# Where the column-half sums of the second chunk's attention outputs are formed, in a four-stage decoder step

## The chip, the cores and the metric

The kernel runs on one core of one Trainium2 chip. The metric is device time in microseconds (us) of one execution. A core has a matrix engine (TensorE, PE in the profile, with PEld for its weight loads), a vector engine (VectorE, DVE), a scalar engine (ScalarE, ACT), GpSimd (POOL), which here mainly issues stores, and SyncE (SP), which here issues loads. The engines run side by side and wait for each other through semaphores.

## The reference, cut to what matters

One inference step for 1024 prompt positions and 8 decode positions, model width 2048, all in fp32:

```
layer A:  u, gate = x @ w_in_a;  d = pool(u) per group @ w_grp
          y = (d * scale * silu(gate)) @ w_out_a;   x = LayerNorm(ALPHA*x + y)
k, v = x @ w_kv
layer B:  q, gate = x @ w_in_b;  o = windowed attention with sinks(q, k, v)
          y = (o * silu(gate)) @ w_out_b;           x = LayerNorm(ALPHA*x + y)
```

The change concerns the gated attention output `o * silu(gate)` of layer B, on its way into the product with `w_out_b`.

## The kernel before

**Tiles and stages.** Activations lie transposed: 128 channels on the partitions, 16 channel tiles side by side, positions along the free dimension. There are two chunks of positions: chunk 0 has 512, chunk 1 has 520, of which the last 8 are the decode positions. The stages run in the order ai (input product of layer A), ao (output product), bi (K, V, query and gate products and attention) and bo (output product of layer B), each for chunk 0 and then chunk 1. `bi` of chunk 1 is followed by `bo` of chunk 0 and that by `bo` of chunk 1, the last stage.

**Products.** Nearly all large products are made in Strassen's way (Winograd's form) with seven products of half size in place of eight: `seven` (L565), its `run` (L619) and the three matmuls of L641 to L643. Each operand is split into a rounded high part (a cast on ACT: L474 for weights, L752 for activations) and a low part (a subtraction on DVE: L489 for weights, L761 for activations); the three matmuls are high times high, high times low and low times high. One product is 24 matmuls, and PE needs its low weights at its third matmul. A stage is 56 products (seven for each of eight pairs of output tiles), and the first two pairs of `bo` share their activations product by product (`both`).

**The activations' sums.** Of the seven activation operands, three are halves of the columns as they are (numbers 0, 4 and 5), and four (1, 2, 3 and 6) are sums and differences of an even channel tile E and an odd one O, each cut into a first column half a and a second column half b:

```python
nc.vector.tensor_sub(t[:, 1, :], E[:, a], E[:, b])
nc.vector.tensor_sub(t[:, 2, :], E[:, b], O[:, b])
nc.vector.tensor_add(t[:, 0, :], O[:, b], t[:, 1, :])
nc.vector.tensor_sub(t[:, 3, :], O[:, a], t[:, 0, :])
```

This is `t_ops` (L803; the four operations are L809 to L812), which also issues the store of the result to a buffer in device memory, `Td`, from POOL (L813; `to` in the profile for these outputs). At the start of the next stage `x_load` (L726, issue L742) loads operands from `act` (`o`) and `Td` (`to`), `x_cast` (L745) makes the high part and `x_make` (L755) the low one. For chunk 0, whose columns are all prompt positions, the gate of an odd tile calls `t_ops` on the two tiles still held in memory. For chunk 1 it can't at once: the half of 260 columns ends with decode columns 512 to 519, which come from another path. So `gate` (L1825) only stores the tile (L1831) and gives its buffer back, and when `bo` of chunk 0 has run 18 products a generator, `t_gen` (L816), starts: it loads the 16 stored tiles again, two at a time (L822), and calls `t_ops` eight times, once a product or less. Its loads, sums and stores thus lie in `bo` of chunk 0. When `bo` of chunk 1 is prepared (`x_begin`, L683, called when the seventh of the eight pairs starts), `ready` runs what is left of the generator to its end.

**Decode columns.** `decode` (L1882) makes the attention of the 8 decode positions for eight tiles at a time; its last step `s9` (L1960, issue L1966) multiplies with the gate values `sgd` and stores 8 columns for 8 tiles.

**Order.** The whole instruction order is written out when the program is made. `begin` (L501) loads, casts and prepares weights some products ahead, as set by `ahead`; `end` (L513) runs the events due after a product (`at` and `product` put them there), the steps of the activations (`x_tick`, L768) and one step of a side generator. PE, DVE and ACT run their instructions in this order, and so do the queues of SP and POOL. There are 53 full buffers (`Mem`, L135), each of which can serve as two halves; `full` hands out the one that was given back longest ago, so the first write to a buffer can wait for a store that still reads it. A second generator, `sum_gen` (L400), makes the sums of `w_out_b` in `bi` of chunk 1 (adds L422, L426 and L427, store L428 of `swob`); it takes a new piece only with more than five free buffers. In `bi` of chunk 1 the prefetch shrinks while fewer than four buffers are free (L504). For two of the eight weight pairs of `bo` chunk 0 the sums are made on the spot (`first_pair`, adds L332).

**The end.** `phase_end` (L1291) uses a small tile `four` for the last four columns of a half.

## Time and profile before

| | |
|---|---|
| median of 3 runs | 2367.28 us (2366.43 to 2371.67) |
| the profiled execution | 2367.62 us, of which the profile's span is 2365.9 us |
| PE busy in the span | 2326.4 us (98%) |
| DVE / ACT / POOL busy | 1923.5 / 1342.2 / 201.5 us |
| granted TensorE clock, mean | 0.996 |
| `t_gen`'s loads of `o` (L822, SP) | x8, first issued at 2063.8, last at 2119.8 |
| stores of `to` (L813, POOL) for both chunks | x16, first issued at 1238.0, last at 2132.8 |

Times on the engines count from the span's start. A row of a group has busy time and the mean of one instruction; a row of waits has the engine and line that waited, the line it waited for, the sum in us, how often, and the longest. A row of a timeline has start, duration, engine, line and operation, and in brackets the idle time ahead of it and what ended that. "PE busy" is modelled from matmul starts, so idle PE is what can be told apart from it.

### The profile page before, as it was taken

To read this page: it belongs to the slowest core of one execution; us is meant where nothing else is said; L and a number is where in the kernel's file an instruction comes from. 1 tells how busy PE (TensorE), PEld (TensorE's weight loads), DVE (VectorE), ACT (ScalarE), POOL (GpSimd) and SP (SyncE) were. 2 spreads that over 40 slices of the span, in tenths; PEclk is the share of its full clock that TensorE was granted. 3 is DMA by queue.
4 is the path that set the end of the run, shared out by engine and by line. 5 is a ranking of instruction groups with operands and counts; after the bars stand their busy time and mean duration, and the time that the engine had idled before them with its cause. 6 is when DMAs were issued, how large, how long until landed. Compare 5 with 4: busy or idle time off the path is not lost. (4 is left out here: it accounts for less than half of the span.)

```text
span 2365.9 us, 46542 instructions
## 1 busy us (share of the span) xinstructions
PE 2326.4 (98%) x18424; PEld 2219.4 (94%) x18424; DVE 1923.5 (81%) x2385; ACT 1342.2 (57%) x2429; POOL 201.5 (9%) x379
## 2 busy tenths in 40 slices
PE   8999999999999999999999999999999999999997
PEld 6899999999999999998778899999999999999997
DVE  8787998776878878868888888887777768888887
ACT  4444446544536547554554656685666667546556
POOL 0111110001000000000111111100000000000000
PEclk9999999999999999999999999999999999999999
DMA  8678789889889989989888766788787768699785
GB/s 294 215 244 303 274 291 349 308 308 315 286 278 365 331 270 324 334 314 330 282 324 322 258 230 224 238 297 275 232 259 221 222 193 298 227 353 371 259 302 194
DMA packets 252059, 669.18 MB, mean 283 GB/s; under 512 B 25760, under 2 KB 106560, under 8 KB 251840
## 3 DMA queue, kind: packets, MB, share of 16 engines
q1 hardware_dynamic: 206368, 501.14, 64.0%
q0 software_dynamic: 45472, 165.07, 17.9%
q8 instruction: 144, 2.36, 0.4%
q14 instruction: 75, 0.61, 0.1%
HBM read 471.01 MB, written 185.59 MB: 278 GB/s over the span
## 5 line engine op out<-in xcount | busy, mean ns | idle before, releaser
L641 PE MATMUL pD<-m,m 128*128 128x260 f32 (+1 forms) x4752 | 1346.9, 283 | 9.9 <-DVE m L602 3.7
L643 PE MATMUL pD<-m,m 128*128 128x260 f32 (+1 forms) x4752 | 1340.5, 282 | 4.5 <-DVE m L489 4.5
L642 PE MATMUL pD<-m,m 128*128 128x260 f32 (+1 forms) x4752 | 1340.3, 282 | 0.0
L641 PEld LDWEIGHTS pD<-m,m 128*128 128x128 f32 x4752 | 896.0, 189 | 21.0 <-issue 10.2
L643 PEld LDWEIGHTS pD<-m,m 128*128 128x128 f32 x4752 | 896.7, 189 | 6.0 <-DVE m L489 6.0
L642 PEld LDWEIGHTS pD<-m,m 128*128 128x128 f32 x4752 | 896.3, 189 | 0.5
L489 DVE TENSOR_TENSOR m<-m,m 128x1024 fp32r<-128x1024 f32 x674 | 814.1, 1219 | 96.1 <-ACT m L474 58.3
L474 ACT CAST m<-m 128x1024 fp32r<-128x1024 f32 x674 | 701.6, 1048 | 305.2 <-DVE m L332 71.3
L669 PE MATMUL pD<-m,m 128*128 128x512 f32 x448 | 179.7, 401 | 8.0 <-ACT m L752 8.0
L670 PE MATMUL pD<-m,m 128*128 128x512 f32 x448 | 177.2, 396 | 0.5 <-DVE m L761 0.5
L671 PE MATMUL pD<-m,m 128*128 128x512 f32 x448 | 177.2, 396 | 0.0
L761 DVE TENSOR_TENSOR m<-m,m 128x1024 fp32r<-128x1024 f32 (+1 forms) x120 | 146.9, 1225 | 7.2 <-ACT m L752 5.7
L614 ACT COPY m<-pD 128x260 f32<-128x260 f32 (+1 forms) x83 | 31.0, 373 | 188.2 <-PE pD L643 188.1
L752 ACT CAST m<-m 128x1024 fp32r<-128x1024 f32 (+1 forms) x120 | 125.7, 1052 | 14.2 <-PE pD L670 5.2
L669 PEld LDWEIGHTS pD<-m,m 128*128 128x128 f32 x448 | 84.7, 189 | 29.9 <-ACT m L752 8.0
L332 DVE TENSOR_TENSOR m<-m,m 128x1024 f32<-128x1024 f32 x88 | 107.6, 1222 | 5.9 <-DMA m<-in_wia 4.2
L670 PEld LDWEIGHTS pD<-m,m 128*128 128x128 f32 x448 | 84.8, 189 | 20.4 <-DVE m L761 1.6
L671 PEld LDWEIGHTS pD<-m,m 128*128 128x128 f32 x448 | 84.6, 189 | 19.8
L602 DVE TENSOR_TENSOR m<-pD,m 128x260 f32<-128x260 f32 (+1 forms) x86 | 36.4, 424 | 81.9 <-PE pD L643 78.6
L1778 ACT ACTIVATE m<-m,sm 128x128 f32<-128x128 f32 x256 | 99.2, 390 | 0.0
L1071 PE MATMUL pD<-m,m 128*128 128x260 f32 (+1 forms) x528 | 91.5, 323 | 0.0
L607 DVE TENSOR_TENSOR m<-pD,m 128x260 f32<-128x260 f32 (+1 forms) x84 | 35.6, 424 | 64.2 <-PE pD L643 64.0
(243 smaller groups left out, 2167.3 us busy)
## 6 DMA issues: line engine op xcount, KB each, us to landing
m<-in_wia SPq DMA_DIRECT2D x124, 512.0 KB
m<-in_wib SPq DMA_DIRECT2D x120, 512.0 KB
swia<-m POOLq DMA_DIRECT2D x64, 512.0 KB, 4.9
m<-swia SPq DMA_DIRECT2D x64, 512.0 KB
m<-swoa SPq DMA_DIRECT2D x64, 512.0 KB
swib<-m POOLq DMA_DIRECT2D x64, 512.0 KB, 5.3
m<-swib SPq DMA_DIRECT2D x64, 512.0 KB
m<-swob SPq DMA_DIRECT2D x56, 512.0 KB
```

Source lines behind the costliest of these rows:

```text
L332: self.nc.vector.tensor_add(s[out].a[:, :1024], s[x].a[:, :1024], s[y].a[:, :1024])
L474: self.nc.scalar.copy(hi.r[:, :1024], self.stream[self.cast].src().a[:, :1024])
L489: self.nc.vector.tensor_sub(lo.r[:, :1024], s.src().a[:, :1024], hi.a[:, :1024])
L641: nc.tensor.matmul(ps[:, :TH], wh[:, s], h, start=new and k == 0, stop=False, skip_group_check=on)
L642: nc.tensor.matmul(ps[:, :TH], wh[:, s], l, start=False, stop=False, skip_group_check=on)
L643: nc.tensor.matmul(ps[:, :TH], wl[:, s], h, start=False, stop=k == 7, skip_group_check=on)
L669: nc.tensor.matmul(ps[:], wh[:, s], h, start=par == 0 and k == 0, stop=False)
L670: nc.tensor.matmul(ps[:], wh[:, s], l, start=False, stop=False)
L671: nc.tensor.matmul(ps[:], wl[:, s], h, start=False, stop=par == 1 and k == 7)
L752: self.nc.scalar.copy(h.r[:, :n], s.a[:, :n])
L761: self.nc.vector.tensor_sub(l.r[:, :n], s.a[:, :n], h.a[:, :n])
L1778: nc.scalar.activation(x["s3"][:, i, :], x["s3"][:, i, :], AF.Exp, bias=nm[:, i : i + 1], scale=0.125, accum_out=rs[:, i : i + 1],)
```

## The change

The generator for chunk 1's attention outputs is no longer added. In its place:

- `gate` of chunk 1 keeps the even tile's half buffer until the odd tile is done, and one product after the odd tile's gate it calls `t_ops` on both, over all 520 columns. Columns 512 to 519 of each tile are set to zero first (a memset on POOL), so the last 8 of the 260 columns of each sum are not the wanted ones.
- `gate` also copies columns 252 to 259 of each tile (the last 8 of the first half) into a new tile `oa` (an ACT copy).
- `o_dec`: when all eight gates of a group of tiles and its `decode` are done, four small DVE operations form the sums of those 8 columns alone, from `oa` and `sgd`, into a new tile `otd`, one product later.
- `x_cast`, for the operands 1, 2, 3 and 6 of this input, copies `otd` over the last 8 columns of the loaded tile (an ACT copy) before the cast.
- `four` in `phase_end` becomes a part of `oa`.

```diff
+TROW = {1: 0, 2: 1, 3: 2, 6: 3}
...
+        self.oa = one.tile([P, NH // 2, NDEC], F32, name="oa")
+        self.otd = one.tile([P, NK // 2, 4, NDEC], F32, name="otd")
+        self.odn = {}
...
         h = self.mem.full()
+        if self.xkey == ("o", 1) and k[0] in TROW:
+            t = s.v(4, THM)[:, :, THM - NDEC : THM]
+            self.nc.scalar.copy(t, self.otd[:, 4 * k[1] : 4 * k[1] + 4, TROW[k[0]], :])
         self.nc.scalar.copy(h.r[:, :n], s.a[:, :n])
...
-        four = self.small(NK * 4, 1)
-        f3 = four[:].rearrange("p (k t) -> p k t", k=NK)
+        four = self.oa[:].rearrange("p k t -> p (k t)")[:, : NK * 4]
+        f3 = four.rearrange("p (k t) -> p k t", k=NK)
...
             nc.gpsimd.dma_start(self.act["o", c][:, t, :TP], a.a[:, :TP])
             if c == 1:
-                self.ao.pop((c, t)).free(True)
-            elif t % 2:
+                nc.gpsimd.memset(a.a[:, TP:T], 0.0)
+                nc.scalar.copy(self.oa[:, t, :], a.a[:, THM - NDEC : THM])
+                self.o_dec(t // 8)
+            if t % 2:
                 e = self.ao.pop((c, t - 1))
-                self.t_ops(e.a[:, :TP], a.a[:, :TP], self.Td["o", c], t // 2, T // 2)
-                e.free(True)
-                self.ao.pop((c, t)).free(True)
+
+                def sums():
+                    self.t_ops(e.a[:, :T], a.a[:, :T], self.Td["o", c], t // 2, T // 2)
+                    e.free(True)
+                    self.ao.pop((c, t)).free(True)
+
+                if c == 1:
+                    self.at(1, sums)
+                else:
+                    sums()
...
+    def o_dec(self, pr):
+
+        self.odn[pr] = self.odn.get(pr, 0) + 1
+        if self.odn[pr] < 9:
+            return
+
+        def go():
+            nc = self.nc
+            d, o = self.sgd[pr][:], self.oa[:, 8 * pr : 8 * pr + 8, :]
+            Ea, Oa, Eb, Ob = o[:, 0:8:2, :], o[:, 1:8:2, :], d[:, 0:8:2, :], d[:, 1:8:2, :]
+            t = self.otd[:, 4 * pr : 4 * pr + 4]
+            nc.vector.tensor_sub(t[:, :, 1, :], Ea, Eb)
+            nc.vector.tensor_sub(t[:, :, 2, :], Eb, Ob)
+            nc.vector.tensor_add(t[:, :, 0, :], Ob, t[:, :, 1, :])
+            nc.vector.tensor_sub(t[:, :, 3, :], Oa, t[:, :, 0, :])
+
+        self.at(1, go)
...
             nc.sync.dma_start(self.act["o", c][:, 8 * pr : 8 * pr + 8, TP:], a3)
+            self.o_dec(pr)
...
-                self.at(18, lambda: add(("o", 1, False), self.t_gen(("o", 1))))
```

More of the change, by code (lines that the diff above doesn't have):

```diff
@@ L737, in x_load @@
             else:
-                src = self.Td[key][:, 4 * g : 4 * g + 4, {1: 0, 2: 1, 3: 2, 6: 3}[i], :]
+                src = self.Td[key][:, 4 * g : 4 * g + 4, TROW[i], :]
         else:
```

## The prediction, made before the change was run

> **What bounds the kernel now.** I read the page's first part, then the busy times by stage, then who PE waited for in each stage, and only then the engines behind those waits. The page first, then the stages from the start of the second chunk's `bi`; columns: stretch, its length, PE, PEld, DVE, ACT and POOL busy with instructions, granted clock, DMA share, GB/s.

> ```profile
> PE 2326.4 (98%) x18424; PEld 2219.4 (94%) x18424; DVE 1923.5 (81%) x2385; ACT 1342.2 (57%) x2429; POOL 201.5 (9%) x379
> ```
> ```profile
> 1590.00:1994.00 404.00, 403.15 (x3608) 391.05 (x3606) 291.95 (x385) 260.61 (x608) 21.93 (x34) 1.00 0.75 238
> 1994.00:2038.00 44.00, 43.98 (x413) 42.24 (x412) 36.42 (x43) 35.45 (x79) 1.08 (x2) 1.00 0.71 241
> 2038.00:2085.00 47.00, 43.81 (x398) 42.36 (x397) 42.36 (x49) 24.22 (x36) 5.90 (x11) 1.00 0.88 305
> 2085.00:2132.00 47.00, 47.00 (x401) 47.00 (x401) 40.15 (x61) 21.39 (x29) 4.78 (x9) 1.00 0.99 354
> 2132.00:2175.00 43.00, 40.43 (x334) 39.58 (x334) 36.55 (x36) 28.00 (x35) 1.59 (x3) 1.00 1.01 361
> ```

> PE is the bound, and the change takes no matmul away. So it can only win idle PE. In the first row, where the sums go, PE idles 0.85 us in 404. In 2085 to 2132, where most of them stand now, it doesn't idle at all, though the DMA engines are full: taking the sums' DVE time out of there is worth nothing by itself. Idle PE lies on either side: 47.00 - 43.81 = 3.2 us before and 43.00 - 40.43 = 2.6 us after. Who it waited for, in these two stretches:

> ```profile
> PE pD L643 <- DVE m L489: 2.5, 4, 1.4
> PE pS L1819 <- DVE m L1805: 0.7, 1, 0.7
> ```
> ```profile
> PE pD L641 <- DVE m L602: 1.0, 1, 1.0
> PE pD L643 <- DVE m L489: 1.0, 1, 1.0
> PE pD L641 <- ACT pD L582: 0.3, 1, 0.3
> PE pD L629 <- ACT m L614: 0.3, 1, 0.3
> ```

> All are waits for weights' low parts or for results to be cleared away, that is for DVE and ACT running late.

> **What the change removes.** Eight 520 KB loads (`o`, L822), with the SP issues; the same sums and stores (`to`, L813) stay but move ahead into `bi`. In 2060 to 2135 (the view of DMA issues):

> ```profile
> m<-o SPq DMA_DIRECT2D x10, 520.0 KB
> to<-m POOLq DMA_DIRECT2D x8, 520.0 KB, 7.6
> ```

> Of these ten loads, eight are the generator's. Why are DVE and ACT late after 2132? Waits of ACT in 2132 to 2153.5, of SP in 2124 to 2150, of DVE in 2132 to 2175, and the two halves of that stretch:

> ```profile
> ACT m L474 <- DMA m<-swob: 4.5, 2, 2.6
> ACT m L474 <- DVE m L489: 2.3, 1, 2.3
> ACT m L474 <- DMA to<-m: 2.3, 1, 2.3
> ACT m L474 <- DMA m<-in_wob: 1.6, 1, 1.6
> ```
> ```profile
> SPq L273 <- DMA to<-m: 6.2, 1, 6.2
> ```
> ```profile
> DVE m L1220 <- ACT m L614: 2.7, 1, 2.7
> ```
> ```profile
> 2142.00:2152.40 10.40, 10.40 (x90) 10.40 (x89) 4.21 (x5) 4.39 (x7) 0.00 (x0) 1.00 1.04 394
> 2152.40:2175.00 22.60, 20.03 (x162) 19.18 (x162) 22.57 (x22) 18.34 (x22) 0.53 (x1) 1.00 1.00 358
> ```

> The order of events: SP's weight load stands 6.2 us behind a buffer whose `to` store is still being read; the loads behind it come in a bunch, with the next stage's inputs, on full DMA engines; ACT waits for `swob` and `in_wob` weights and for one more `to` store; L614, which clears the last product away, stands behind these casts, so DVE idles 2.7 us; then DVE works 22.57 of 22.60 us and PE waits 20.03 of 22.60. Three of the four waits here (1.0 + 1.0 + 0.3 = 2.3 us) hang on this. The fourth, L629, is the start of a second-chunk stage and I leave it. With the generator gone, the buffer wait and some 8.5 MB (16 x 520 KB) of 2060 to 2135's traffic go; at 354 GB/s that is 24 us of DMA time, and DVE, 2.7 us earlier, is no longer behind. **Term 1: -2.3 us**; bounds 0 (weights late for the inputs' sake alone) and -2.6 (all four waits). What is late next is DVE at the inputs' low parts, still without a gap until 2175.

> **What it adds in `bi`.** Seven of the eight sums. One sum costs DVE the distance from its first operation to what follows it; here one of the old ones:

> ```profile
> 2085.55 0.43 DVE L809 TENSOR_TENSOR m<-m 128x260 f32<-128x260 f32 x1
> 2085.90 0.42 DVE L810 TENSOR_TENSOR m<-m 128x260 f32<-128x260 f32 x1
> 2086.24 0.42 DVE L811 TENSOR_TENSOR m<-m,m 128x260 f32<-128x260 f32 x1
> 2086.70 0.43 DVE L812 TENSOR_TENSOR m<-m,m 128x260 f32<-128x260 f32 x1
> 2087.05 0.42 DVE L607 TENSOR_TENSOR m<-pD,m 128x256 f32<-128x256 f32 x1
> ```

> 2087.05 - 2085.55 = 1.5 us, seven times 10.5 us. DVE has 404 - 292 = 112 us idle there, one sum per 50 us or so, so PE's work hides them; without that cover they would cost 10.5. ACT gets 16 copies of eight columns and POOL 16 memsets; the nearest rows:

> ```profile
> L1864 ACT COPY sgd<-m 128x16 f32<-128x16 f32 x8 | 1.6, 201 | 0.0
> L1006 POOL MEMSET m<- 128x15 f32 x16 | 1.8, 115 | 30.3 <-PE pD L642 9.6 <-DVE m L722 7.8 <-DMA g<-m 5.7
> ```

> 16 x 0.20 = 3.2 us of ACT against 143 us idle, 16 x 0.12 = 1.8 us of POOL. The waits that they add: ACT's copy waits for the gate (DVE), and behind it stand weight casts that are two or three products ahead of PE; DVE's sum waits for the memset, which stands in POOL's queue behind the tile's store, itself only waiting for the gate, one product earlier. Eight stores of `to` join POOL's queue, where a `swob` store may stand behind one; nobody on PE's path waits for it soon. **Term 2: 0**; bounds 0 and +1.4 (one new wait as long as the longest of the rows above).

> **What it adds in `bo` of chunk 0.** The last two tiles' attention runs late: the gate of tile 15 and the last step of the second `decode` stand here.

> ```profile
> 2051.82 0.69 DVE L1828 SCALAR_TENSOR_TENSOR m<-pS,m 128x512 f32<-128x512 f32 x1 [1.35 <-PE pS L1944]
> 2058.97 0.23 DVE L1962 SCALAR_TENSOR_TENSOR sgd<-pS,sgd 128x64 f32<-128x64 f32 x1 [0.87 <-PE pS L1953]
> ```

> So the eighth sum falls at about 2056 and the second `o_dec` at about 2061, in the stretch where PE waited 2.5 us for L489 and DVE has no other gap than these two until 2083. Four dependent small operations follow each other as these do:

> ```profile
> 2039.54 0.16 DVE L1929 SCALAR_TENSOR_TENSOR sm<-sm,prm 128x1 f32<-128x1 f32 x1
> 2039.74 0.16 DVE L1930 TENSOR_TENSOR sm<-prm,sm 128x1 f32<-128x1 f32 x1
> ```

> 0.2 us apart, 0.7 to 0.8 for four. Added: 1.5 + 0.7 = 2.2 us of DVE; the gap of 0.87 ahead of L1962 absorbs that much of the sum; 1.3 us reaches L489 and, since PE already waits there, PE. **Term 3: +1.3 us**; bounds 0 (the products catch up) and +2.2 (no gap absorbs). [...]

> **At the start of the last stage** ACT copies `otd` into 8 of the 14 inputs, 8 x 0.2 = 1.6 us, perhaps half of it by 2175, where ACT has 22.6 - 18.3 = 4.3 us free. **Term 4: 0**, bounds 0 and +0.8. The end of the kernel keeps its instructions.

> **Sum**: -2.3 + 0 + 1.3 + 0 = -1.0 us on the profiled execution's 2367.62 us (0.34 above the median of the runs), so 2366.6 for it and 2366.3 for the median.

> **Rivals.**

> *A, the slow one: the held buffers push the sums of `w_out_b` back.* An even tile's half buffer is now held until the odd tile's sum, about half of the time, and `sum_gen` takes a piece only with more than five buffers free. That it already goes short of them shows in its stores, at times 29 us apart; the last one is issued at 1893:

> ```profile
> 1817.71 0.72 POOL L428 DMA_DIRECT2D swob<-m  x1 [8.21 <-DVE m L427]
> 1846.82 0.71 POOL L428 DMA_DIRECT2D swob<-m  x1 [12.02 <-DMA o<-sgd]
> ...
> 1893.13 0.71 POOL L428 DMA_DIRECT2D swob<-m  x1 [7.11 <-DVE m L427]
> ```

> If pieces slip by more than 2038 - 1893 = 145 us they land in the stretch where DVE has nothing left, at (from the groups by line)

> ```profile
> L422 DVE TENSOR_TENSOR m<-m 128x512 f32<-128x512 f32 x56 | 38.3, 684 | 0.0
> L427 DVE TENSOR_TENSOR m<-m 128x256 f32<-128x256 f32 x56 | 23.8, 426 | 1.9
> ```

> 0.68 + 2 x 0.43 = 1.5 us each (L426 is of L427's shape). Four of them are +6.1: 2366.3 + 6.1 = 2372.4. Below that slip they cost nothing, since DVE has idle time. For it: the shortage; against it: 145 us of slack are five such long steps, and half a buffer is held, not several.

> *B, the weights stay late.* The 14 inputs and the weights alone fill the DMA engines after 2132 (share 1.01), so term 1 is 0: 2367.3 + 1.3 = 2368.6.

> *C, both stretches clear.* With the DVE work, the loads and the buffer waits gone, prefetch gets so far ahead that PE waits neither in 2038 to 2085 nor after 2132: -(3.2 + 2.6) = -5.8, 2361.5. Against it: in the first of these stretches the change adds DVE work.

> **How the numbers follow.** Forecast (terms near their values, 2363 to 2370) 0.46; A 0.22; B 0.17; C 0.15. A difference of 0.2%, 4.7 us, is about what a measurement of this kernel can tell from no change. C is beyond it (0.15 faster), A is beyond it on the other side (0.22 slower), the forecast and B lie within (0.63). The terms' own bounds give -2.6 to +4.4 and so 2364.7 to 2371.7; the range is widened to C's time below and past A's above: 2361.5 to 2373.5, with a few per cent of C and some of A (more than four pieces) outside.

> **What would show it.** Term 1: no wait of SP for `to` stores near 2130, no 2.7 us gap of DVE before L1220, and PE idle of about 0.3 in place of 2.6 us in the last pair. Term 3: PE's waits for L489 between the gate of tile 15 and the next 25 us grow from 2.5 to nearly 4 us. Term 2: PE idle in `bi` stays below 1 us. A: stores of `swob` from L428 after the first load of `w_out_b`, and DVE without gaps around them. B: ACT still waiting for weights after `x_begin`. The prediction is wrong in kind if PE's idle time changes by more than 2 us outside these two stretches.

## The result, and the profile after

The changed kernel takes 2383.79 us (median, 2382.83 to 2384.99), the kernel before 2367.32 us (2366.43 to 2371.67): 1.0067 times as long, 95% interval 1.0057 to 1.0077. The prediction was 2366.3 us, with a range up to 2373.5. It is slower by 16.5 us and lies outside the range.

The page of the kernel after, its first part; then its stretches, with the columns of the prediction's table (the first is the same stretch; the others run between the same matmuls as 2038 to 2085, 2085 to 2132 and 2132 to 2175 before):

```profile
PE 2329.5 (98%) x18424; PEld 2222.2 (93%) x18424; DVE 1924.9 (81%) x2393; ACT 1344.9 (56%) x2453; POOL 203.3 (9%) x395
```
```profile
1590.00:1994.00 404.00, 391.66 (x3446) 379.18 (x3445) 284.49 (x394) 248.09 (x598) 26.10 (x52) 0.99 0.71 229
...
2055.21:2103.14 47.93, 44.09 (x398) 42.30 (x397) 44.25 (x57) 25.28 (x37) 6.53 (x13) 1.00 0.86 297
2103.14:2150.37 47.23, 47.23 (x402) 47.23 (x401) 31.60 (x32) 20.32 (x30) 1.06 (x2) 1.00 0.76 256
2150.37:2191.06 40.69, 39.66 (x334) 39.27 (x333) 34.32 (x33) 29.22 (x40) 1.06 (x2) 1.00 0.90 303
```

The page hardly differs: PE is 98% busy in both, DVE and ACT as before. The stages tell it. In `bi` of chunk 1, where PE idled 0.85 us of 404, it now idles 404 - 391.66 = 12.3 us, and it issues 3446 matmuls in place of 3608. Who PE waits for there:

```profile
PE pD L645 <- ACT pD L586: 8.8, 4, 3.0
PE pS L1749 <- DVE m L1721: 2.4, 2, 1.4
PE pD L647 <- DVE m L493: 1.2, 1, 1.2
```

Four of the seven pauses are waits for ACT, three are waits for DVE. (Lines after: L645 to L647 are the three matmuls, L586 the ACT operation that was L582, L478 the weights' cast, L493 their low part, L618 was L614, L816 to L819 are the sum, L1835 the gate, L1841 the copy of decode columns.) The gates give the measure used below, the time from tile 1's gate to tile 15's. Before, from 1704.56 (tile 15's row, 2051.82, stands in the prediction), and after:

```profile
1704.56 0.68 DVE L1828 SCALAR_TENSOR_TENSOR m<-pO,m 128x512 f32<-128x512 f32 x1
```
```profile
1703.75 0.68 DVE L1835 SCALAR_TENSOR_TENSOR m<-pO,m 128x512 f32<-128x512 f32 x1
...
2068.97 0.69 DVE L1835 SCALAR_TENSOR_TENSOR m<-pS,m 128x512 f32<-128x512 f32 x1 [1.33 <-PE pS L1978]
```

347.26 us before and 365.22 after: **17.96 us are lost while the sums are made**, which is all of the slowdown and a little more. The rest went as forecast: from tile 15's gate to the end the changed kernel is 1 us ahead. That the place is the sums' can be seen by following one. Before, at tile 1, ACT's cast finds DVE done and nothing waits:

```profile
1708.97 1.32 DVE L1763 COPY_PREDICATED m<-mki,pS 128x1024 f32<-128x1024 int32 x1
...
1710.65 1.05 ACT L474 CAST m<-m 128x1024 fp32r<-128x1024 f32 x1
...
1711.89 2.54 DVE L489 TENSOR_TENSOR m<-m,m 128x1024 fp32r<-128x1024 f32 x2
...
1713.64 0.36 ACT L582 ACTIVATE pD<-pD 128x260 f32<-128x260 f32 x1
```

After, at the same tile (the timelines of DVE, ACT and PE):

```profile
1708.18 1.31 DVE L1770 COPY_PREDICATED m<-mki,pS 128x1024 f32<-128x1024 int32 x1
1709.52 1.22 DVE L1774 TENSOR_REDUCE sm<-m 128x8 f32<-128x1024 f32 x1
...
1711.06 0.42 DVE L816 TENSOR_TENSOR m<-m 128x260 f32<-128x260 f32 x1
...
1712.20 0.43 DVE L819 TENSOR_TENSOR m<-m,m 128x260 f32<-128x260 f32 x1
1712.55 0.42 DVE L430 TENSOR_TENSOR m<-m 128x256 f32<-128x256 f32 x1
...
1713.34 1.22 DVE L493 TENSOR_TENSOR m<-m,m 128x1024 fp32r<-128x1024 f32 x1
...
1714.59 1.05 ACT L478 CAST m<-m 128x1024 fp32r<-128x1024 f32 x1 [4.65 <-DVE m L493]
...
1717.19 0.36 ACT L586 ACTIVATE pD<-pD 128x260 f32<-128x260 f32 x1
...
1717.61 0.39 PE L645 MATMUL pD<-m,m 128*128 128x260 f32 x1 [2.34 <-ACT pD L586]
```

DVE does the next tile's masking and its maximum (L1770 and L1774), the sum (1711.06 to 1712.63) and two operations on a piece of `w_out_b`, and only then the weight's low part. ACT's cast starts 0.03 us after that low part ends (1713.34 + 1.22): a cast takes nothing from a low part and waits for one only where it writes a buffer that the low part reads, so this cast was left with the buffer that this very L493 gives back. ACT stands for 4.65 us; behind the cast in its queue are four exponentials and then L586, which PE needs. PE stands for 2.34 us. Over the stretch 1700 to 1994, ACT's casts waited for low parts this long, before and after:

```profile
ACT m L474 <- DVE m L489: 5.4, 4, 2.1
```
```profile
ACT m L478 <- DVE m L493: 30.6, 12, 4.9
```

**And the pauses cost more than their length.** PE in the 6 us behind three of its pauses (2.34, 2.95 and 2.06 us) and behind a shorter one (1.42 us, second pair of rows); columns: PE busy with matmuls, granted clock, DMA share, GB/s:

```profile
1717.61:1720.61 3.00, 3.00 (x19) 0.75 0.88 280
1720.61:1723.61 3.00, 3.00 (x20) 0.68 0.87 285
1771.26:1774.26 3.00, 3.00 (x25) 1.00 0.77 281
1774.26:1777.26 3.00, 3.00 (x28) 1.00 1.00 279
1826.79:1829.79 3.00, 3.00 (x19) 0.76 0.91 232
1829.79:1832.79 3.00, 3.00 (x20) 0.67 0.78 247
1882.09:1885.09 3.00, 3.00 (x17) 0.65 0.99 307
1885.09:1888.09 3.00, 3.00 (x23) 0.78 0.36 118
```

Behind the longer pauses the clock is granted at 0.65 to 0.78 for 6 us, and the rows count 39, 39 and 40 matmuls where they count 53 behind the short one (a matmul that runs across the border of two rows is counted in both; by starts it is 37, 37 and 38 against 50). What this costs can be read exactly, since both kernels run the same 18424 matmuls in the same order and the two traces can be laid beside each other, start by start. Between the two gates the matmuls that end a pause come 13.5 us later in the kernel after, a pause of 0.85 us that only the kernel before has gives back 1.0, the 6 us behind the three longest pauses add 5.0 and all else 0.5: together the 17.96 that were measured.

### The profile page after: what moved, and what is told of

Read it like the earlier page. It is cut to its first block, busy times and chain, and to the rows that moved or that the text cites. A ratio compares the mean times of both kernels' runs of the same rounds, so it can differ in the third digit from the quotient of the medians.

```text
span 2382.1 us, 46610 instructions
## 1 busy us (share of the span) xinstructions
PE 2329.5 (98%) x18424; PEld 2222.2 (93%) x18424; DVE 1924.9 (81%) x2393; ACT 1344.9 (56%) x2453; POOL 203.3 (9%) x395
## 3 DMA queue, kind: packets, MB, share of 16 engines
q0 software_dynamic: 45472, 165.07, 17.9%
## 5 line engine op out<-in xcount | busy, mean ns | idle before, releaser
L645 PE MATMUL pD<-m,m 128*128 128x260 f32 (+1 forms) x4752 | 1349.0, 284 | 16.8 <-ACT pD L586 11.2
L647 PE MATMUL pD<-m,m 128*128 128x260 f32 (+1 forms) x4752 | 1342.6, 283 | 5.4 <-DVE m L493 5.4
L645 PEld LDWEIGHTS pD<-m,m 128*128 128x128 f32 x4752 | 897.5, 189 | 28.6 <-ACT pD L586 12.6
L647 PEld LDWEIGHTS pD<-m,m 128*128 128x128 f32 x4752 | 898.4, 189 | 7.3 <-DVE m L493 7.3
L493 DVE TENSOR_TENSOR m<-m,m 128x1024 fp32r<-128x1024 f32 x674 | 814.8, 1220 | 108.8 <-ACT m L478 60.1
L646 PEld LDWEIGHTS pD<-m,m 128*128 128x128 f32 x4752 | 898.1, 189 | 0.5
L478 ACT CAST m<-m 128x1024 fp32r<-128x1024 f32 x674 | 701.2, 1048 | 308.3 <-DVE m L493 71.0
L618 ACT COPY m<-pD 128x260 f32<-128x260 f32 (+1 forms) x83 | 31.0, 374 | 191.1 <-PE pD L647 191.0
L673 PEld LDWEIGHTS pD<-m,m 128*128 128x128 f32 x448 | 84.6, 189 | 29.9 <-ACT m L759 8.1
L606 DVE TENSOR_TENSOR m<-pD,m 128x260 f32<-128x260 f32 (+1 forms) x86 | 36.5, 424 | 89.5 <-PE pD L647 89.4
L674 PEld LDWEIGHTS pD<-m,m 128*128 128x128 f32 x448 | 84.7, 189 | 20.7 <-DVE m L768 2.0
L675 PEld LDWEIGHTS pD<-m,m 128*128 128x128 f32 x448 | 84.6, 189 | 19.7
L1078 PEld LDWEIGHTS pD<-m,m 128*128 128x128 f32 x528 | 79.5, 188 | 8.2
```

Source lines behind the costliest of these rows:

```text
L478: self.nc.scalar.copy(hi.r[:, :1024], self.stream[self.cast].src().a[:, :1024])
L493: self.nc.vector.tensor_sub(lo.r[:, :1024], s.src().a[:, :1024], hi.a[:, :1024])
L645: nc.tensor.matmul(ps[:, :TH], wh[:, s], h, start=new and k == 0, stop=False, skip_group_check=on)
L646: nc.tensor.matmul(ps[:, :TH], wh[:, s], l, start=False, stop=False, skip_group_check=on)
L647: nc.tensor.matmul(ps[:, :TH], wl[:, s], h, start=False, stop=k == 7, skip_group_check=on)
L673: nc.tensor.matmul(ps[:], wh[:, s], h, start=par == 0 and k == 0, stop=False)
```

## The experiments

Each total is that of one profiled execution; the kernel before took 2365.97 beside e1 to e4, 2368.26 beside e5 to e7, 2366.75 beside e8 to e10, 2367.07 (median) beside e11 and e12, and 2368.70 beside e13 to e15. Since such totals differ by some us between executions (the kernel before: 2366.43 to 2371.67), the loss is read inside each trace, from tile 1's gate to tile 15's, less 347.26. One kernel that ran twice this way gave 1.04 and 1.32.

| run | total, us | loss, us | casts waiting for low parts, us (times) |
|---|---|---|---|
| the changed kernel | 2383.97 | 17.96 | 30.6 (12) |
| e1 even half not held | 2379.16 | 12.36 | 24.1 (10) |
| e2 hold alone | 2366.56 | -0.94 | 6.1 (7) |
| e3 sum at once | 2372.24 | 5.87 | 20.6 (10) |
| e4 copies late | 2381.29 | 15.82 | 27.2 (11) |
| e5 sum later | 2392.71 | 26.61 | 23.1 (9) |
| e6 DVE work alone | 2370.75 | 2.30 | 11.0 (7) |
| e7 one operation a product | 2371.07 | 3.55 | 16.1 (11) |
| e8 sum on POOL | 2380.22 | 13.39 | 24.6 (10) |
| e9 plain return | 2373.67 | 6.79 | 3.0 (3) |
| e10 at once, plain, late | 2366.23 | 1.04 | 4.3 (3) |
| e11 buffer order alone | 2369.04 | 3.40 | 13.6 (7) |
| e13 order and DVE work | 2381.83 | 13.15 | 22.0 (8) |
| e14 order and store | 2370.60 | 2.88 | 13.6 (7) |
| e15 order, DVE work, store | 2387.71 | 18.17 | 28.7 (11) |

The first theories were four: the hold of the half buffers (H), the sum's place on DVE (D, from e5 on called place), ACT's copies (C), and, from e5 on, the sum's store.

**e1 and e2, the hold.** In e1 the even tile's half is given back at its gate, and the sum is made of the odd tile alone:

```diff
+            if c == 1 and t % 2 == 0:
+                self.ao.pop((c, t)).free(True)
...
-                e = self.ao.pop((c, t - 1))
+                e = self.ao.pop((c, t - 1)) if c == 0 else a
```

> The changed kernel, but the even tile's half buffer is given back at its own gate, as in the kernel before; the sums stand where the change puts them, with the same DVE, POOL and ACT work, formed from the odd tile twice (so their values, and the decode columns' place in them, are not the wanted ones). Theory H (buffers: the held half takes away the free buffer that a weight cast on ACT would have used, so the cast waits for DVE's last read of a buffer only just given back, and the PSUM copy L586 that PE needs stands behind it): the some 17.9 us lost in bi of chunk 1 fall to 0 to 4 us. Rival D (DVE: 1.5 us of sums right behind the softmax maximum delay the weights' low part, whatever the buffers): the loss stays at 15 to 18 us. Rival C (ACT stands in its queue behind the copy into oa, which waits for the gate): it stays at 15 to 18 us too.

e2 is the kernel before with only the hold added:

```diff
-            if c == 1:
-                self.ao.pop((c, t)).free(True)
+            if c == 1 and t % 2:
+                def give():
+                    self.ao.pop((c, t - 1)).free(True)
+                    self.ao.pop((c, t)).free(True)
+                self.at(1, give)
```

> The kernel before, with one thing of the change alone: the even tile's half buffer (and the odd one's) is held until one product after the odd tile's gate. No sums, memsets or copies there; the generator in bo of chunk 0 stays. Theory H: bi of chunk 1 loses 5 to 15 us against the kernel before, and nothing comes back later. Rivals D and C: within 1 us of the kernel before in that stage.

Loss 12.36 and -0.94. The hold by itself costs nothing, so as the one cause it falls. e1 says less than it seems: its loss lies between the two forecasts, and it is in good part another loss. One pause of PE there is 6.6 us long, behind a low part that waits for the store of a sum; the changed kernel has no such pause in this stretch:

```profile
1824.56 2.54 DVE L493 TENSOR_TENSOR m<-m,m 128x1024 fp32r<-128x1024 f32 x2 [4.76 <-DMA to<-m]
```

Every later run that loses much holds the halves too, so whether the hold has a share beside the other causes isn't shown.

**e3 and e4, place and copies.** e3 calls `sums()` in the odd gate's own event (and the memset ahead of the gate); e4 makes both tiles' copies in `sums`, one product later.

> The changed kernel with the sums in the odd gate's own event in place of one product later, and the memset ahead of the gate, so that it is done by then. DVE then does the sums ahead of the softmax maximum and not between it and the weights' low part; the even half is held one product less. Theory H: the loss in bi stays above 10 us, since the even half is held nearly as long. Rival D, in the form that the place decides: it falls below 5 us. Rival C: it stays.

> The changed kernel with both tiles' copies into oa made together with the sums, one product after the odd gate, when the gate is done and ACT needn't wait for it. The same copies, the same hold, the same sums. Rival C: the loss in bi falls from some 17.9 to below 5 us. Theories H and D: it stays within 3 us of 17.9.

Losses 5.87 and 15.82. Moving the sum takes away two thirds of the loss, though not down to the 5 us that D allowed, and it also moves the moment at which the sum's buffers are taken and given back. Moving the copies takes away some 2 us (17.96 - 15.82), so C falls.

**e5, e6, e7: place against store.** e5 has `self.at(3, sums)` in place of `self.at(1, sums)`.

> The changed kernel with the sum three products after the odd tile's gate instead of one. Place (the sum stands on DVE behind the two maxima of the next tile and ahead of the weights' low parts, and there every us that they come late grows into a pause of PE): three products after the gate the maxima are over, the sum is 1.5 us beside the low parts alone, and up to tile 15's gate 0 to 6 us are lost instead of 17.9: 2366 to 2372. Store (the sum's full buffer, given back with its store in flight, makes the next taker wait wherever the sum stands): the same 15 to 18 us, 2381 to 2384.

Both were wrong: 26.61 lost. One sum of e5 in the timelines, POOL and DVE, then ACT and PE:

```profile
1715.59 0.55 POOL L820 DMA_DIRECT2D to<-m  x1 [0.69 <-DVE m L819]
...
1722.15 1.23 DVE L493 TENSOR_TENSOR m<-m,m 128x1024 fp32r<-128x1024 f32 x1 [6.87 <-DMA to<-m]
...
1723.41 1.04 ACT L478 CAST m<-m 128x1024 fp32r<-128x1024 f32 x1 [8.03 <-DVE m L493]
...
1724.78 0.39 PE L645 MATMUL pD<-m,m 128*128 128x260 f32 x1 [3.50 <-ACT m L595]
```

The store leaves at 1715.59, and a low part takes the same buffer next and waits 6.87 us for it, ACT behind DVE, PE behind ACT. So the store can matter, and later isn't better.

e6 is e2 with the DVE work added, into a tile of its own:

```diff
...
+                    y, lo, hi = self.scr, slice(0, P * 2), slice(P * 2, P * 4)
+                    nc.vector.tensor_sub(y[:], e.a[:, lo], e.a[:, hi])
+                    nc.vector.tensor_sub(y[:], e.a[:, hi], a.a[:, hi])
+                    nc.vector.tensor_add(y[:], a.a[:, hi], y[:])
+                    nc.vector.tensor_sub(y[:], a.a[:, lo], y[:])
```

> The kernel before, with the two halves held until one product after the odd gate and there four DVE operations of 128x256 into a small tile of their own; their results are not used, there is no full buffer, no store, no memset and no copy for them, and the sums in bo of chunk 0 stay. Place: 10 to 18 us lost up to tile 15's gate, total 2376 to 2384. Store: 0 to 3 lost, 2366 to 2369.

e7 makes the four operations in four events, with the same buffers and store, the full buffer and the odd half being held three products longer:

```diff
...
+                    for n in range(4):
+                        self.at(1 + n, lambda n=n: part(n))
```

> The changed kernel with the sum's four operations one a product, at one to four products after the odd gate; the same buffers (one held three products longer) and the same store. Place: no product's low part is more than 0.43 us late for it, 0 to 5 us lost up to tile 15's gate, 2365 to 2370. Store: 12 to 18 lost, 2378 to 2384.

2.30 and 3.55: e6 speaks against the place alone, e7 against the store alone. Neither theory holds by itself. What the two share is that they take away one half of a pair: e6 leaves the full buffers alone, e7 doesn't put 1.5 us in front of a low part.

**A third theory, lock step.** It comes from two lines of the kernel:

```python
i = min(self.whole(), key=lambda i: max(self.f[i]))       # Mem.full
self.mem.release(self, 10 if stored else 0)               # Slot.free
```

`free(True)` marks a buffer as if given back ten releases later, so that a store in flight can end. A sum takes the buffer that has been free longest and gives back that one and the two halves, all marked. (The kernel before marks its halves too; the full buffer is new.) With few buffers free, the next casts are left with the one that the low part just ahead of them has given back; cast and low part then wait for each other in turn, and whatever delays DVE there delays ACT.

**e8, e9, e10.** e8 has the four operations as `nc.gpsimd` ones; e9 has one edit; e10 makes the sum at once and copies and returns later:

```diff
-                    e.free(True)
-                    self.ao.pop((c, t)).free(True)
+                    e.free(c == 0)
+                    self.ao.pop((c, t)).free(c == 0)
```
```diff
...
+                def copies():
+                    for u, h in ((t - 1, e), (t, self.ao.pop((c, t)))):
+                        nc.scalar.copy(self.oa[:, u, :], h.a[:, THM - NDEC : THM])
+                        self.o_dec(u // 8)
+                        h.free()
```

> The changed kernel with the sum's four operations on POOL instead of DVE, at the same place, with the same buffers, returns and store. A third theory, lock step: the sum takes the buffer that has been free longest and gives back three with a mark that puts them ten releases later; the next weights' casts are left with the buffer that the last L493 gave back, so cast and L493 wait for each other in turn, and there each us that DVE spends on the sum reaches PE; it takes both, the order of the buffers and the work on DVE. Lock step: without the work on DVE 4 to 9 us lost up to tile 15's gate, 2369 to 2375. Place (DVE's work alone): 0 to 3 lost, 2366 to 2369. Store: 15 to 18 lost as before, 2380 to 2384.

> The changed kernel with one thing other: the sum gives its two half buffers back without the mark that puts them ten releases later (their own stores were issued a product or more earlier); the same instructions at the same place, the full buffer with its mark as it was. Lock step: the casts find a buffer that has been free for longer, 0 to 5 us lost up to tile 15's gate instead of 17.9, 2366 to 2371. Place and store: nothing changes for them, 15 to 18 lost, 2380 to 2384.

> The changed kernel with three edits: the sum in the odd gate's own event (memset ahead of the gate), both tiles' copies of decode columns one product later, and the two halves given back after them without the mark. Lock step: 0 to 2 us lost, and with the 2.2 gained at the start of the last stage 2365 to 2368. Place or store: as with the sum at once alone, about 6 lost, less some 2 for the copies, 2370 to 2373.

e9 keeps every instruction of PE, DVE and ACT in its place and only takes the mark off two halves: 6.79 in place of 17.96, above the 0 to 5 of lock step and far below the 15 to 18 of the others, and the casts wait 3.0 us for low parts in place of 30.6. e10 loses 1.04 (forecast 0 to 2). e8 misses: 13.39 where 4 to 9 were expected. It isn't a clean taking away: the fourth operation stood on POOL behind a `swob` store, the `to` store went out late, and a low part took its buffer:

```profile
1712.77 0.74 POOL L432 DMA_DIRECT2D swob<-m  x1 [5.23 <-DVE m L431]
1713.47 0.81 POOL L1855 TENSOR_TENSOR m<-m,m 128x260 f32<-128x260 f32 x1
1714.60 0.57 POOL L1856 DMA_DIRECT2D to<-m  x1 [0.31 <-POOL m L1855]
...
1721.73 1.23 DVE L493 TENSOR_TENSOR m<-m,m 128x1024 fp32r<-128x1024 f32 x1 [8.29 <-DMA to<-m]
```

**e11, e13, e14, e15: building the loss up from the kernel before.** To e2's `give` are added a full buffer taken and given back with the mark (e11), and to that the DVE work (e13), the store (e14), or both (e15):

```diff
                 def give():
+                    s = self.mem.full()
+                    nc.gpsimd.memset(s.a[:, :NDEC], 0.0)
+                    s.free(True)
```

In place of the memset, e13 has e6's four operations, with `y = s.v(4, P * 2)` as their result; e14 sets all of `s` to zero and stores it; e15 has the four operations and stores `y`:

```diff
+                    nc.gpsimd.memset(s.v(4, THM), 0.0)
+                    nc.gpsimd.dma_start(self.Td["o", c][:, t // 2], s.v(4, THM))
```

> The kernel before, with the two halves held until one product after the odd gate as in the hold alone, and there a full buffer taken, eight columns of it set to zero by POOL, and given back at once with the mark; no sum, no store, no copy, and the sums in bo of chunk 0 stay. The buffers are so taken in the same order as in the changed kernel. If that order alone makes casts and L493 wait for each other, 8 to 13 us are lost up to tile 15's gate, 2374 to 2380; if it takes a sum's work or a store in flight as well, 0 to 3, 2366 to 2369.

> The kernel before with the buffer order of the changed one, as in the buffer alone (3.4 us lost), and the four DVE operations of 128x256 as in the DVE work alone (2.3 lost), their result in the full buffer, which is given back at once with the mark; no store, no copies, the sums in bo of chunk 0 stay. Lock step that takes order and DVE work together: 10 to 16 us lost up to tile 15's gate, 2377 to 2383. If the two only add: 5 to 7, 2371 to 2374, and the rest of the 17.9 is the store.

> The kernel before with the buffer order of the changed one, and the buffer (set to zero by POOL over 128x1040) stored to `to`, one product after each odd gate; no sum, no copies, the sums in bo of chunk 0 stay. Store: 10 to 16 us lost up to tile 15's gate, 2377 to 2383. Lock step: 3 to 5, as with the buffer alone, 2368 to 2371.

> The kernel before with all three, the order of the buffers, the four DVE operations and the store of their result; no copies, the sums in bo of chunk 0 stay. By any theory that names these three as the cause, 14 to 18 us lost up to tile 15's gate, 2380 to 2385; if it is less than 10, the generator's absence from bo or the memset and the copies have a share that these runs have not shown.

Order alone 3.40, which neither end of e11's forecast had; DVE work alone 2.30; **both together 13.15**, more than twice their sum of 5.70. The nearest base for these three is e2: in e11 the instructions of PE, DVE and ACT stand in the order of e2, and e6 and e13 add 32 DVE operations to it and nothing else on these engines, while the kernel before has some casts and sums elsewhere, because the prefetch and `sum_gen` go by how many buffers are free. From e2's -0.94 the order costs 4.34, the DVE work 3.24, and both together 14.09. The waits of ACT and of PE say how, e11 first, then e13:

```profile
ACT m L474 <- DVE m L489: 13.6, 7, 3.5
...
PE pD L641 <- ACT pD L582: 2.6, 3, 1.5
```
```profile
ACT m L474 <- DVE m L489: 22.0, 8, 4.9
...
PE pD L641 <- ACT pD L582: 8.3, 4, 2.9
```

The order alone chains ACT to DVE, and three PE pauses result, none longer than 1.5 us; 1.5 us of DVE work at the same points makes the longest 2.9 us. The store adds nothing without the DVE work (2.88), and 5 us with it (18.17 - 13.15); with it the loss of the changed kernel is made up, just above the 14 to 18 expected (the total, 2387.71, lies above the 2385 too). Its own wait shows once in e15, and once in the changed kernel too:

```profile
DVE m L489 <- DMA to<-m: 5.2, 1, 5.2
```
```profile
1886.88 1.23 DVE L493 TENSOR_TENSOR m<-m,m 128x1024 fp32r<-128x1024 f32 x1 [5.49 <-DMA to<-m]
```

**e12, e10 again, timed.**

> The kernel with the sum at once, the copies one product later and the halves given back without the mark, again and timed: 2366.2 in its one run so far. Lock step: 0.998 to 1.001 of the kernel before (2.2 gained at the start of the last stage, some 1 lost in bi, some 1 in bo of chunk 0); by the place or the store theory 1.001 to 1.003.

Median 2370.45 us (2367.65 to 2373.20) against 2367.07: ratio 1.0013, interval 1.0004 to 1.0023. So even the best arrangement found doesn't win. The median lies just above lock step's 0.998 to 1.001 and inside the 1.001 to 1.003 of the place or store theory, so this total doesn't speak for lock step. The profiled execution was the fastest of its eleven; where the others lose their 3 us isn't shown. Inside its trace the loss in `bi` is 1.32.

## Why the prediction was wrong

- **Term 2, the step that failed**: "DVE has 404 - 292 = 112 us idle there, one sum per 50 us or so, so PE's work hides them", at 0 with +1.4 as the upper bound. Measured: 17.96. The idle time is an average. At the one place where the sum was put, one product behind the odd gate, DVE is already working off the next tile's masking and maximum, and a low part that ACT needs stands right behind; the sum's size was right (1711.06 to the next operation at 1712.55, 1.49 us, against 1.5) and its cover wasn't there.
- In the same step: "behind it stand weight casts that are two or three products ahead of PE". Being ahead didn't help a cast that had no buffer (tile 1's stood 4.65 us for L493). e9, e11 and e13 show that the buffers' order is one half of the cause; the bound "one new wait as long as the longest of the rows" had no term for one engine's delay being handed on through buffers, sum after sum.
- **No term for the clock.** A pause of PE was priced at its length. Three of them also cost 5.0 us in the 6 us behind them, at a granted clock of 0.65 to 0.78.
- **Rival A** had the right sign and the right object (held buffers, free ones short), but another mechanism: sums of `w_out_b` slipping past 2038. The last of their stores went from 1893 to 1934, far from there, and e2 shows that the hold by itself is free.
- **Term 3, right**: +1.3 forecast. From tile 15's gate (17.15 us behind) to the last wait of PE for L493 (2090.81, which was at 2072.53: 18.28 behind) 1.1 are lost. PE's waits grew from 2.5 to 3.2 us, not quite to the "nearly 4" of the text.

```profile
PE pD L647 <- DVE m L493: 3.2, 5, 1.3
PE pS L1826 <- DVE m L1812: 0.7, 1, 0.7
```

- **Term 1, right in kind**: -2.3 forecast, -2.2 measured (18.28 behind at 2090.81, 16.09 at L633's matmul, 2188.66). That the numbers meet is partly luck: laid start by start, the three waits that are gone gave 2.6, and the wait at the start of the second-chunk stage, which the prediction left alone (L629, 0.3 us), took back 0.7, with 0.3 spread over the rest. That wait is PE's only wait in 2150 to 2191:

```profile
PE pD L633 <- ACT m L618: 1.0, 1, 1.0
```

Every run without the generator shows this wait alone (0.5 to 1.0 us); e2 and e6, which keep it, have 2.3 us in three waits and 3.2 us in four. SP's wait for a `to` store is gone. Its other two signs failed: PE idles 1.0 us and not about 0.3, and the 2.7 us gap of DVE is still there as two of 1.7 us ahead of L1227, without harm. Which of load, store or DVE work of the generator gave the 2.2 us wasn't tried apart.
- **Term 4, right**: 0; nothing lies between 2191 and the end that wasn't there before (the shift stays at 16.1 to 16.2 us).

What stays open: why e5's sums meet their stores so much more often, and the rest of e9's 6.79 us, in which the DVE work (2.30) and the copies (2.1, from e4) account for some 4.4. Even the copies' 2.1 is doubtful, since e15 loses as much as the changed kernel without any.

## What to carry to other kernels

Price added work on an engine at the place where it is queued: look there for what stands ahead of and behind it, and not at the engine's idle time over the stage. Where buffers come from a short list, ask for every buffer that the change takes or marks which one the next user is left with, and whose last reader that one waits for. Two changes that cost 2 and 3 us alone cost 13 together here, so test them together as well as apart.

## What the runs showed of the hardware

In the trace of after a short pause of PE cost most of its length again in clock: behind pauses of 2.34, 2.95 and 2.06 us the next 6 us took some 1.65 us longer each than the same matmuls before. In all 17 traces, from 40 to 2340 us, no pause of up to 1.83 us was followed by a lower granted clock and each of more than 2.56 us was; between them it went either way: a pause of 1.94 us ahead of the same matmul was followed by 0.72 over 6 us in before (from 360.74) and by 1.00 in after (from 360.84), one of 1.95 us in e9 by 0.62 over 3 us, and one of 2.10 us in e12 and one of 2.56 us in e11 by 1.00.

```profile
1715.70:1719.11 3.41, 1.50 (x12) 1.50 (x13) 0.66 (x1) 1.86 (x10) 0.00 (x0) 1.00 0.97 304
1719.11:1722.52 3.41, 3.41 (x18) 3.41 (x17) 1.96 (x3) 2.81 (x11) 0.00 (x0) 0.50 0.82 276
```
```profile
1359.09:1362.50 3.41, 2.44 (x21) 2.24 (x19) 3.41 (x4) 2.75 (x11) 0.53 (x1) 1.00 0.06 12
1362.50:1365.91 3.41, 1.82 (x15) 1.85 (x16) 3.41 (x4) 1.52 (x8) 0.00 (x0) 1.00 0.80 261
1365.91:1369.32 3.41, 3.41 (x32) 3.41 (x31) 3.34 (x7) 1.76 (x3) 1.07 (x2) 1.00 0.58 177
```

The two readings of the clock behind the 2.34 us pause agree: in the 6 us from 1717.61, 3 x 0.25 + 3 x 0.32 = 1.71 us of clock are missing, which is half speed for 3.4 us, and the one step at 0.50 is 3.41 us long.
